# A weighted sum of experts on one core: the stores of ten tokens on ScalarE's queue or on SyncE's

## The chip, the cores and the metric

The kernel runs on 1 core of one Trainium2 chip. A core has five engines with instruction streams of their own: TensorE (PE), VectorE (DVE), ScalarE (ACT), GpSimd (POOL) and SyncE (SP). Transfers between the device's memory and the on-chip memory are done by 16 DMA engines; here SP issues them. The metric is the device time of one execution in microseconds (us). Six runs of the kernel before gave a median of 709.88 us, from 709.42 to 710.2.

## The reference

For each of 16 x 1024 tokens there are 8 expert outputs of 512 numbers and 8 weights. The result is the weighted sum over the experts, all in float32.

```python
def setup_inputs():
    batch, seq, n_experts, expert_dim = 16, 1024, 8, 512
    ...

def reference(expert_outputs, combine_weights):
    weights = combine_weights[..., np.newaxis]
    return np.sum(expert_outputs * weights, axis=2).astype(np.float32)
```

That is 268 MB to read and 33.5 MB to write.

## The kernel before

A token of each of the 128 partitions makes one step of the work: 16,384 tokens are 128 per partition, and "token" from here on means one token in all 128 partitions. It has 16 KB per partition to load (2 MB in all) and 2 KB to store (256 KB in all). 120 tokens are done in 12 rounds (`ROUNDS`) of ten (`R`), which a loop of six passes on DVE runs two at a time; the last 8 tokens (`TAIL`) are done apart.

`ring` holds the loaded rows of ten tokens; a round's tokens are loaded in chunks of 4, 4 and 2 (`CHUNKS`), each into the slots of the same tokens of the round before. `acc` holds the sums of twenty tokens, one half for even rounds and one for odd (`h`). The instruction streams are written out by hand, one function for each engine, and ordered by semaphores alone:

- SP, `loads_and_stores` (L94): for each round the three loads (L107), each after DVE has finished the tokens whose slots it overwrites (`done` counts finished tokens), and then, from round 1 on, the store of the round before (`store`, L95 to L100; its transfer is issued at L98), after `done` has reached all of that round's tokens. This is the value for which the third load waited already. Then come the eight single loads of the tail (L119), the store of round 11 (L120), and four stores of the tail's tokens, of 4, 2, 1 and 1 tokens (L123). Transfers of one issuing engine go into one queue.
- ACT, `weights` (L139): a copy of the weights of each round from `w_t`, which holds all of them, to `w_c` (L145), which holds two rounds' worth; from round 2 on after DVE has finished the round whose half is overwritten. Then 32 diagonal matrices for the tail (L150).
- DVE, `terms` (L170): for each round it waits for the weights, for the half of `acc` to be stored (`stored[h]`), and for each chunk's load (all through `take`, L172); then, for pairs of tokens, one product (L203) and seven multiply-adds (L186) for each token. For the tail it adds four terms of each token (L186) to four that PE has summed.
- PE, `first_terms` (L155): for each tail token four products by diagonal matrices, summed in PSUM (L162).
- POOL makes an identity matrix, once.

Of the kernel before, what the change touches and what calls it, by code (L numbers as in the profile page):

```python
# [10 lines left out]
def kernel(  # L11
# [17 lines left out]
    nc = tc.nc  # L29
# [6 lines left out]
    R = 10  # L36
# [5 lines left out]
    ROUNDS = LOOP // R  # L42
# [10 lines left out]
    o_g = o[0:cut].rearrange("(n p g) d -> n p g d", p=P, g=G)  # L53
# [17 lines left out]
    acc = one.tile([P, G, D], fp32, name="acc")  # L71
# [10 lines left out]
    stored = [sem(f"stored{h}") for h in range(2)]  # L82
    step = sem("step")
    done = sem("done")
# [6 lines left out]
    def load_of(j):  # L91
        return [k for k, (q, m) in enumerate(tail_loads) if q <= j < q + m][0]

    def loads_and_stores(sync):  # L94
        def store(n):  # L95
            h = n % 2
            sync.wait_ge(done, (n + 1) * R)
            sync.dma_start(  # L98
                out=o_g[n // 2, :, h * R : h * R + R], in_=acc[:, h * R : h * R + R]
            ).then_inc(stored[h], 16)  # L100

        for n in range(ROUNDS):
            for c, (r, m) in enumerate(CHUNKS):
                if n:
                    sync.wait_ge(done, (n - 1) * R + r + m)
                g = n % 2 * R + r
                sync.dma_start(  # L107
                    out=ring[:, r : r + m], in_=x_g[n // 2, :, g : g + m]
                ).then_inc(loaded[c], 16)
                if n == 0 and c == 0:  # L110
                    sync.dma_start(
                        out=w_t[:, 0:LOOP].rearrange("p (n g) e -> p n g e", g=G), in_=w_g
                    ).then_inc(w_in, 16)
                    sync.dma_start(out=w_t[:, LOOP:T_P], in_=w_x).then_inc(w_in, 16)
            if n:
                store(n - 1)
        for k, (j, m) in enumerate(tail_loads):
            sync.wait_ge(done, LOOP - R + j + m)
            sync.dma_start(out=ring[:, j : j + m], in_=x_t[:, j : j + m]).then_inc(tail_in[k], 16)  # L119
        store(ROUNDS - 1)  # L120
        for j, m in tail_stores:
            sync.wait_ge(done, LOOP + j + m)
            sync.dma_start(out=o_t[:, j : j + m], in_=acc[:, j : j + m]).then_inc(tail_out, 16)  # L123
        sync.wait_ge(stored[(ROUNDS - 1) % 2], 16)
        sync.wait_ge(tail_out, 16 * len(tail_stores))

    def identity(gpsimd):
        gpsimd.memset(ident, 0.0).then_inc(id_set, 1)  # L128
        gpsimd.affine_select(  # L129
            out=ident,  # L130
            in_=ident,
            compare_op=mybir.AluOpType.not_equal,
            fill=1.0,
            base=0,
            pattern=[[-1, P]],
            channel_multiplier=1,
        ).wait_op(id_set, 1, "sem-ge").then_inc(id_set, 1)

    def weights(scalar):  # L139
        scalar.wait_ge(w_in, 32)  # L140
        for n in range(ROUNDS):
            if n >= 2:
                scalar.wait_ge(done, (n - 1) * R)
            h = n % 2
            scalar.copy(  # L145
                out=w_c[:, h * R : h * R + R], in_=w_t[:, n * R : n * R + R]
            ).then_inc(w_set[h], 1)
        scalar.wait_ge(id_set, 2)
        for k, (j, e) in enumerate(diags):
            i = scalar.mul(out=diag[:, k % DIAGS], in_=ident, mul=w_t[:, LOOP + j, e : e + 1])  # L150
            i.then_inc(diag_set, 1)
            if k >= DIAGS:
                i.wait_op(product, k - DIAGS + 1, "sem-ge")

    def first_terms(tensor):  # L155
        came = set()
        for k, (j, e) in enumerate(diags):
            if load_of(j) not in came:
                came.add(load_of(j))
                tensor.wait_ge(tail_in[load_of(j)], 16)  # L160
            tensor.wait_ge(diag_set, k + 1)
            tensor.matmul(  # L162
                ps[:, j],
                lhsT=diag[:, k % DIAGS],
                rhs=ring[:, j, e],
                start=e == 0,
                stop=e == pe_e[j] - 1,
            ).then_inc(product, 1)
# [58 lines left out]
            count(i, j, e)  # L227

    with tc.tile_critical(no_gpsimd_drain=True):  # L229
        loads_and_stores(nc.sync)  # L230
        identity(nc.gpsimd)
        weights(nc.scalar)
        first_terms(nc.tensor)
        terms(nc.vector)

# [29 lines left out]
```

## Time and profile before

| | |
|---|---|
| median of 6 runs | 709.88 us (709.42 to 710.2) |
| the profiled execution | 709.67 us |
| its span, first to last instruction | 707.9 us |
| DMA engines, mean rate over the span | 427 GB/s |
| loads L107, issue to landing | 22.0 to 50.9 us, median 33.4 |
| stores L98, issue to landing | 30.7 to 39.5 us, median 38.7 |
| tail loads L119, issue to landing | 30.1 to 35.0 us, median 32.5 |

A row of the next table is a group of instructions of one line and form: line, engine, operation, output<-inputs, count | busy us, mean ns of one | idle time just before them, and what ended most of it.

```profile
L186 DVE SCALAR_TENSOR_TENSOR acc<-ring,w_c,acc 128x512 f32<-128x512 f32 x840 | 561.4, 745 | 0.0
L203 DVE TENSOR_SCALAR acc<-ring,w_c 128x512 f32<-128x512 f32 x120 | 52.6, 480 | 65.8 <-DVEq L172 65.8
L162 PE MATMUL ps<-ring,diag 128*128 128x512 f32 x64 | 32.5, 660 | 666.7 <-DMA ring<-in_expert_outputs_dram 666.7
L145 ACT COPY w_c<-w_t 128x80 f32<-128x80 f32 x12 | 3.0, 257 | 556.9 <-DVE acc L186 534.6
L150 ACT ACTIVATE diag<-ident,w_t 128x128 f32<-128x128 f32 x32 | 12.4, 399 | 119.5 <-PE ps L162 119.5
```

DVE's 840 and 120 instructions are the rounds; a pair of tokens takes some 10.06 us, a round of ten 50.3 us. Idle time of an engine that is not the bottleneck costs nothing. SPq and DVEq stand for the instruction queues of SP and DVE, where waits and issues are seen. The trace also keeps a record of every DMA packet (queue, size, start, duration) and of each of the 16 steps by which a transfer counts its semaphore up when it lands, one for each DMA engine.

### The profile page before, as it was taken

Reading aid. Unit: us, or ns where it says so; the run is one execution under the profiler, and the core shown is the slowest. Engines: PE = TensorE matmul, PEld = TensorE weight load, DVE = VectorE, ACT = ScalarE, POOL = GpSimd, SP = SyncE. Lnnn points to the kernel's source line nnn. Section 1 sums busy time; section 2 is a strip of 40 time slices with the busy share of each in tenths; the row PEclk is TensorE's granted clock in tenths of the full one; section 3 lists DMA queues with packets and bytes.
Section 4 is the critical chain, followed back from the end, with each engine's and each line's share of the span. In section 5 each row is a group of like instructions: output and inputs, shape, how many; then the busy total and the mean of one; then the engine's idle time right before and its main releaser. Section 6 shows DMA issues by size and latency. Waiting matters only on the chain. (4 is left out here: it accounts for less than half of the span.)

```text
span 707.9 us, 1388 instructions
## 1 busy us (share of the span) xinstructions
PE 32.5 (5%) x64; PEld 12.9 (2%) x64; DVE 628.1 (89%) x992; ACT 16.6 (2%) x45; POOL 0.7 (0%) x6
## 2 busy tenths in 40 slices
PE   0000000000000000000000000000000000000674
PEld 0000000000000000000000000000000000000221
DVE  0599999899799799799799799799799799899974
ACT  0000000000000000000000000000000000000230
POOL 0000000000000000000000000000000000000000
PEclk9999999999999999999999999999999999999998
DMA  9999999999999999999999999999999999999997
GB/s 411 389 471 418 415 421 438 463 396 463 422 411 448 430 420 454 444 411 448 415 431 435 455 407 459 418 420 439 441 420 450 437 413 446 426 424 427 431 424 302
DMA packets 9570, 302.53 MB, mean 427 GB/s; under 512 B 1120, under 2 KB 1888, under 8 KB 2272
## 3 DMA queue, kind: packets, MB, share of 16 engines
q1 hardware_dynamic: 9568, 302.52, 99.3%
q14 instruction: 2, 0.02, 0.0%
HBM read 268.96 MB, written 33.55 MB: 427 GB/s over the span
## 5 line engine op out<-in xcount | busy, mean ns | idle before, releaser
L186 DVE SCALAR_TENSOR_TENSOR acc<-ring,w_c,acc 128x512 f32<-128x512 f32 x840 | 561.4, 745 | 0.0
L203 DVE TENSOR_SCALAR acc<-ring,w_c 128x512 f32<-128x512 f32 x120 | 52.6, 480 | 65.8 <-DVEq L172 65.8
L162 PE MATMUL ps<-ring,diag 128*128 128x512 f32 x64 | 32.5, 660 | 666.7 <-DMA ring<-in_expert_outputs_dram 666.7
L162 PEld LDWEIGHTS ps<-ring,diag 128*128 128x128 f32 x64 | 12.9, 211 | 685.4 <-DMA ring<-in_expert_outputs_dram 671.5
L186 DVE SCALAR_TENSOR_TENSOR acc<-ring,w_t,acc 128x512 f32<-128x512 f32 x24 | 17.6, 750 | 0.6
L145 ACT COPY w_c<-w_t 128x80 f32<-128x80 f32 x12 | 3.0, 257 | 556.9 <-DVE acc L186 534.6
L150 ACT ACTIVATE diag<-ident,w_t 128x128 f32<-128x128 f32 x32 | 12.4, 399 | 119.5 <-PE ps L162 119.5
L186 DVE SCALAR_TENSOR_TENSOR acc<-ring,w_t,ps 128x512 f32<-128x512 f32 x8 | 5.9, 745 | 7.8 <-PE ps L162 7.8
L145 ACT ACT_TABLE_LOAD x1 | 1.3, 1283 | 0.9 <-SPq L229 0.9
L129 POOL TENSOR_SCALAR_AFFINE_SELECT ident<-ident 128x128 f32<-128x128 f32 x1 | 0.3, 292 | 0.1
L128 POOL MEMSET ident<- 128x128 f32 x1 | 0.2, 204 | 0.5 <-SPq L229 0.5
L249 POOL MEMSET const-bfloat16-1.0<- 128x1 bf16 x1 | 0.1, 102 | 0.0
L249 POOL MEMSET const-uint8-127<- 128x1 uint8 x1 | 0.1, 102 | 0.0
L249 POOL MEMSET const-float32-0.0<- 128x1 f32 x1 | 0.1, 99 | 0.2 <-issue 0.2
L249 POOL MEMSET const-float32-1.0<- 128x1 f32 x1 | 0.1, 99 | 0.0
## 6 DMA issues: line engine op xcount, KB each, us to landing
ring<-in_expert_outputs_dram SPq DMA_DIRECT2D x12, 4096.0 KB, 33.0
out_dram<-acc SPq DMA_DIRECT2D x12, 2560.0 KB, 38.7
ring<-in_expert_outputs_dram SPq DMA_DIRECT2D x8, 2048.0 KB, 32.5
out_dram<-acc SPq DMA_DIRECT2D x1, 1024.0 KB, 19.1
out_dram<-acc SPq DMA_DIRECT2D x1, 512.0 KB, 9.4
out_dram<-acc SPq DMA_DIRECT2D x2, 256.0 KB, 5.4
w_t<-in_combine_weights_dram SPq DMA_DIRECT2D x1, 480.0 KB, 22.7
ring<-in_expert_outputs_dram SPq DMA_DIRECT2D x24, 33.7
```

Source lines behind the costliest of these rows:

```text
L128: gpsimd.memset(ident, 0.0).then_inc(id_set, 1)
L129: gpsimd.affine_select(out=ident, in_=ident, compare_op=mybir.AluOpType.not_equal, fill=1.0, base=0, pattern=[[-1, P]], channel_multiplier ...
L145: scalar.copy(out=w_c[:, h * R : h * R + R], in_=w_t[:, n * R : n * R + R]).then_inc(w_set[h], 1)
L150: i = scalar.mul(out=diag[:, k % DIAGS], in_=ident, mul=w_t[:, LOOP + j, e : e + 1])
L162: tensor.matmul(ps[:, j], lhsT=diag[:, k % DIAGS], rhs=ring[:, j, e], start=e == 0, stop=e == pe_e[j] - 1,).then_inc(product, 1)
L186: return vector.scalar_tensor_tensor(out=acc[:, g], in0=ring[:, g % R, e], scalar=weight, in1=before, op0=mult, op1=add)
L203: i = vector.tensor_scalar_mul(out=acc[:, g], in0=ring[:, g % R, 0], scalar1=weight)
L249: nc = _bacc.Bacc("TRN2", target_bir_lowering=False, num_devices=1)
```

## The change

The stores of rounds 0 to 10 move from SP's stream to ACT's. `store` becomes a function of the queue. On ACT, the store of round n-2 stands ahead of the copy of round n's weights and takes over its wait (the same value of `done`); the store of round 10 stands after the last copy and ahead of the diagonal matrices. On SP the loads of all rounds and of the tail now follow one another, and behind them are the store of round 11 and the four stores of the tail, 18 tokens in all, as before. Waits, transfers, their sizes and the work of the other engines are the same.

```diff
-    def loads_and_stores(sync):
-        def store(n):
-            h = n % 2
-            sync.wait_ge(done, (n + 1) * R)
-            sync.dma_start(
-                out=o_g[n // 2, :, h * R : h * R + R], in_=acc[:, h * R : h * R + R]
-            ).then_inc(stored[h], 16)
-
+    def store(queue, n):
+        h = n % 2
+        queue.wait_ge(done, (n + 1) * R)
+        queue.dma_start(
+            out=o_g[n // 2, :, h * R : h * R + R], in_=acc[:, h * R : h * R + R]
+        ).then_inc(stored[h], 16)
+
+    def loads_and_last_stores(sync):
...
-            if n:
-                store(n - 1)
...
-        store(ROUNDS - 1)
+        store(sync, ROUNDS - 1)
...
-    def weights(scalar):
+    def weights_and_stores(scalar):
         scalar.wait_ge(w_in, 32)
         for n in range(ROUNDS):
             if n >= 2:
-                scalar.wait_ge(done, (n - 1) * R)
+                store(scalar, n - 2)
             h = n % 2
             scalar.copy(
                 out=w_c[:, h * R : h * R + R], in_=w_t[:, n * R : n * R + R]
             ).then_inc(w_set[h], 1)
+        store(scalar, ROUNDS - 2)
         scalar.wait_ge(id_set, 2)
```

More of the change, by code (lines that the diff above doesn't have):

```diff
@@ L229 @@
     with tc.tile_critical(no_gpsimd_drain=True):
-        loads_and_stores(nc.sync)
+        loads_and_last_stores(nc.sync)
         identity(nc.gpsimd)
-        weights(nc.scalar)
+        weights_and_stores(nc.scalar)
         first_terms(nc.tensor)
```

## The prediction

> **What bounds the kernel now.** I read the page's first parts, then the waits, the chain of waits, the timeline around one store, and last the DMA packet records. From the page, in order: span; busy time by engine; DMA busy share in 40 slices; DMA queues; DMA issues with KB and us to landing.
>
> ```profile
> span 707.9 us, 1388 instructions
> PE 32.5 (5%) x64; PEld 12.9 (2%) x64; DVE 628.1 (89%) x992; ACT 16.6 (2%) x45; POOL 0.7 (0%) x6
> ...
> DMA  9999999999999999999999999999999999999997
> ...
> q1 hardware_dynamic: 9568, 302.52, 99.3%
> ...
> ring<-in_expert_outputs_dram SPq DMA_DIRECT2D x12, 4096.0 KB, 33.0
> out_dram<-acc SPq DMA_DIRECT2D x12, 2560.0 KB, 38.7
> ```
>
> The DMA engines are the bound: 99.3% of the span is packets of one queue. DVE has 80 us to spare. A transfer lands 33 to 39 us after its issue, so it spends most of that behind others.
>
> The waits (us in total, times, longest) show where DVE's slack lies, and that ACT is idle:
>
> ```profile
> DVE acc L203 <- DVEq L172: 65.8, 11, 25.1
> ...
> DVE acc L186 <- PE ps L162: 7.8, 4, 4.1
> ...
> ACT w_c L145 <- DVE acc L186: 534.6, 10, 54.8
> ```
>
> 25.1 us is the first load; the other 40.7 us are one wait of about 4.1 us in each of ten rounds, ended by the load of tokens 0 to 3.
>
> The chain of waits (start, us, what) at its end:
>
> ```profile
> 660.78 34.68 DMA ring<-in_expert_outputs_dram
> 695.46 0.04 issue
> 695.50 3.71 PE ps L162 x8
> ...
> 701.60 0.75 DVE acc L186
> ```
>
> The end hangs on the last tail load, at 695.46; PE, DVE and the last store's 4.1 us follow.
>
> The timeline around the store of round 10:
>
> ```profile
> 616.33 0.33 SPq L107 DMA_DIRECT2D ring<-in_expert_outputs_dram  x1
> 616.70 0.43 SPq L98 DMA_DIRECT2D out_dram<-acc  x1
> 620.39 0.88 DVE L203 TENSOR_SCALAR acc<-ring,w_c 128x512 f32<-128x512 f32 x2 [4.09 <-DVEq L172]
> ```
>
> At the store's issue three loads stand ahead of it: the last 3.6 us of tokens 0-3 of round 11 (landing at 620.25), tokens 4-7 (639.61) and 8-9 (649.31). The store landed at 655.39.
>
> The packet records give the price of one row on one engine: 2418 ns for 64 KB (chunks of four tokens), 1213 for 32 KB, 761 for a store's 20 KB row, 611 for 16 KB. Each transfer is 8 rows per engine. All are near 27 GB/s an engine, in either direction, and they stand end to end.
>
> **The change, part by part.**
>
> *Removed from SP, added to ACT:* 11 store issues of 432 ns and their 11 waits. SP waits 583 us of the span anyway. ACT gains 11 x 0.43 = 4.8 us against 534.6 us of idle. Queued behind each wait is the copy of w_c, which before waited for the same value of `done`; it starts 0.43 us later, needed some 50 us later: 0. The diagonals now stand behind the store of round 10 (616.7 instead of 561.97); PE first needs them at 660.29: 0, while 43 us of cover last. POOL, PE and DVE issue the same.
>
> *Bytes:* the same 302.5 MB. Stores 0 to 10 are done before the last load in either kernel. Loads plus these stores are what the engines do until 695.46, so order alone leaves that moment where it is: 0.
>
> *Where the stall goes:* the store now starts at 616.7 instead of some 649. Its 8 rows x 0.76 = 6.1 us fall into the load of tokens 4-7, which had 640.53 - 639.61 = 0.9 us to spare on DVE, so DVE waits some 5 us there. The next round's tokens 0-3 land as before, so the 4.1 us wait at L203 vanishes: one wait for another, and DVE runs some 5 us later. At the end DVE idles 7.8 us on PE before the last token, which takes up the 5. Without that cover each us over 7.8 would count fully. Later DVE means later load issues: when DVE has finished tokens 0-3 and frees their slots, the 5 us of tokens 4-7 that it then waits for and 9.7 us of tokens 8-9 (649.31 - 639.61) are still queued, 14.7 us (before: 9.7 + 6.1 of the store, less 0.9). When it frees tokens 4-7, the next round's tokens 0-3 still have some 9 us to go (14 before). So the engines do not run dry: 0. If they did, each us of it would count fully. The 18 late tokens' stores stay on SP: 0.
>
> *What the trace does not show:* two long transfers on two queues taking turns on an engine. The Trainium skill, page "DMA: Bandwidth & Descriptors", section "Queues, rings and completion order", says that an engine takes turns between the queues by packet. If a record is such a packet, each store makes 8 switches to and fro in place of one; no row here shows that. The same page's "Rules for kernel authors" speaks against this change: spreading DMAs over SP and ACT brings no bandwidth, they interleave on the same engines. Read as free interleaving, that makes the time 709.9.
>
> My own count is 8 pairs of switches for each store, 7 more than now, 77 in all, because rows alternate if both queues are served alike. Rows for one pair:
> - Same queue, load to store to load: from the landing of tokens 0-3 in round 8 to that in round 11, three periods. The first engine to land took 54.45 us a round, the eighth 54.50. Packets alone are 16 x 2418 + 8 x 1213 + 8 x 761 + 4 x 9 ns, less 3.5 ns overlap each: 54.39. A pair costs 0.06 to 0.11 us. Over nine rounds from round 2 the last engine lost 0.25.
> - Other queue: twice an instruction fetch of queue 14 (309 and 333 ns) cut into the load stream. The next load packet took 1835 instead of 1213 ns and 1273 instead of 611: 0.62 to 0.66 us lost besides the fetch itself.
>
> Low end for a pair: a gain, if the second queue fills what switches now cost the last engine, 0.25 x 11 = 2.8 us. Overlap of both directions is not excluded either. High end: 0.64 x 88 = 56 us. I take 0.08, the late rounds of the same pair of transfers, since those are the very operations, and a fetch into instruction memory is not. 77 x 0.08 = 6.2 us.
>
> **Sum:** span 707.9 and what lies around it 1.8 make this execution's 709.67; the median is 709.88, 0.2 higher. 709.9 + 0 + 0 + 6.2 = 716.1; I say 716.
>
> **Rivals.**
> - *Free turns:* the rule as read above, or the store served only after the queued loads, so that the change does nothing. For it: the same rate in both directions and no gaps. Against: both pairs of rows show some loss, and 1.4 us over 88 turns is only 0.016 us each. Time 709.9, 708.5 to 711.3.
> - *The other side, the second queue fills the engines' losses:* at the last load the first engine ended at 691.29, the last at 695.46. Of these 4.2 us some 3 grew at the switches up to round 11 (the first engine landed that round's tokens 0-3 at 617.04, the last at 620.25). If one queue moves while the other turns, 2.8 us go: 707. If reads and writes overlap on an engine, more: 11 x 6.06 = 66.7 us of store packets. It decides from 2% overlap of those (1.4 us). With all hidden DVE binds: 25.1 to its start, 12 rounds of five pairs at 10.06 (the timeline's 630.47 to 640.53), 23.5 of tail, 4.1 for the last store and 3.2 from its landing at 706.4 to 709.67 = 660. Against: equal rates of load and store look like one shared path.
> - *Dear turns:* each return to the load queue costs what it cost after the fetch, 709.9 + 56 = 766, or half of that, 738. For it: the only two rows in which a queue was left and resumed. Against: both were fetches, and may be slow at their own target.
>
> **How the numbers follow.** A run of this kernel ranges from 709.42 to 710.2, so 0.2% (1.4 us) is about what can be told from no change. Cheap turns (711.3 to 722): 0.42. Dear or half-dear turns (above 722): 0.20. Free turns or nothing done: 0.13. Filled or overlapped: 0.25. So faster 0.25, same 0.13, slower 0.62. The likeliest case by itself spans 711.5 to 722. The range goes down to 706.5, which takes in the 2.8 us, and leaves some 0.07 for real overlap below; up to 735, which leaves some 0.13 for dear turns above.
>
> **What would show it.** Store to landing: 38.7 us before; with alternating rows some 8 x (2.42 + 0.76) = 25 us, with equal bytes some 12. DVE's wait: about 5 us at tokens 4-7 instead of 4.1 at tokens 0-3, its sum little changed when turns are cheap. Load packets next to store packets longer than 2418 ns or with gaps: their sum over 16 engines is my 6.2 us. A first-to-last spread at the last load below 4.2 us speaks for the filled losses; a span under 706 for overlap. I am wrong if the DMA share falls well below 99% (engines run dry), or if the end no longer hangs on the last tail load but on DVE.

## The result and the profile after

The changed kernel takes 708.24 us (median of 18 runs, 707.74 to 708.81); the kernel before took 709.86 us in the same comparison (38 runs, 709.25 to 710.2). The ratio is 0.9978, with a 95% interval of 0.9972 to 0.9984: 1.6 us faster, just past what can be told from no change. I had forecast 716, some 6 us slower. The profiled execution took 708.63 us, against 709.67 before.

From the page of the changed kernel: span, busy time by engine, DMA busy share, DMA queues, and DMA issues with KB and median us to landing.

```profile
span 706.8 us, 1388 instructions
PE 31.0 (4%) x64; PEld 12.2 (2%) x64; DVE 628.1 (89%) x992; ACT 16.7 (2%) x45; POOL 0.7 (0%) x6
...
DMA  9999999999999999999999999999999999999997
...
q1 hardware_dynamic: 7984, 273.68, 89.8%
q10 hardware_dynamic: 1584, 28.84, 9.5%
...
out_dram<-acc ACTq DMA_DIRECT2D x11, 2560.0 KB, 25.9
```

The engines are as full as before, now from two queues (89.8 + 9.5 = 99.3%). A store lands 25.9 us after its issue instead of 38.7. The time to look for is 1 us in 707, so it will not be found in shares.

DVE's waits in the changed kernel (us in total, times, longest):

```profile
DVE acc L202 <- DVEq L171: 69.1, 13, 25.0
DVE acc L185 <- PE ps L161: 3.4, 2, 1.8
```

Without the first load's 25.0 us DVE waits 44.1 us in the rounds (40.7 before) and 3.4 in the tail (7.8). The timeline around the store of round 10 shows where:

```profile
619.83 0.33 SPq L107 DMA_DIRECT2D ring<-in_expert_outputs_dram  x1
619.84 0.36 ACTq L97 DMA_DIRECT2D out_dram<-acc  x1
...
643.96 0.88 DVE L202 TENSOR_SCALAR acc<-ring,w_c 128x512 f32<-128x512 f32 x2 [4.01 <-DVEq L171]
```

Load and store are now issued in the same moment by two engines. DVE's wait of 4 us stands 24 us behind the store, at tokens 4 to 7, no longer right behind it, at tokens 0 to 3. The chain of waits at the end of the changed kernel (start, us, what):

```profile
664.21 30.17 DMA ring<-in_expert_outputs_dram
694.37 0.04 issue
694.42 3.71 PE ps L161 x8
...
700.52 0.75 DVE acc L185
```

The last tail load lands at 694.37 instead of 695.46. That is 1.1 us, the whole difference between the spans. Everything behind it is the same.

The packet records say why it lands earlier. Packets that follow one another on one engine, found by matching each start to an end (bytes, start in us, ns), show the turns:

```
65536 137.915  2418
20480 140.329   761
65536 141.087  2418
20480 143.501   761
65536 144.258  2418
20480 146.672   761
```

One row of a load, one row of a store, each as long as it is alone and each starting as the one ahead of it ends (they overlap by 4 ns). This is the rule that I cited of the Trainium skill ("DMA: Bandwidth & Descriptors", "Queues, rings and completion order"); the "packet" of its turns is here a single row, 64 KB or 20 KB. I call "loss" what packets take beyond the usual time of their size, summed over all packets and divided by 16 engines. The last load's landing is given for the eighth and the last of the 16 engines.

| profiled execution | loss 73 to 127 us (first store) | loss 127 to 660 us | last load, eighth engine | last engine |
|---|---|---|---|---|
| before | 0.34 | 1.39 | 692.22 | 695.46 |
| before_again | 0.39 | 1.16 | 691.94 | 695.39 |
| after | 0.53 | 0.41 | 691.32 | 694.37 |
| after_again | 0.44 | 0.41 | 691.16 | 694.76 |

The first engine to land its last load, at 691.0 to 691.3 us, is hardly moved. The others had fallen behind it at the stores, and hardly do any more once the first store is past. In the round of the first store both kernels lose, the changed one on 64 KB rows beside the first store rows that took up to 3076 ns instead of 2418; no run shows why.

### The profile page after: what moved, and what is told of

It is laid out like the page before. It is cut to its first block, busy times and chain, and to the rows that moved or that the text cites. A ratio compares the mean times of both kernels' runs of the same rounds, so it can differ in the third digit from the quotient of the medians.

```text
span 706.8 us, 1388 instructions
## 1 busy us (share of the span) xinstructions
PE 31.0 (4%) x64; PEld 12.2 (2%) x64; DVE 628.1 (89%) x992; ACT 16.7 (2%) x45; POOL 0.7 (0%) x6
## 3 DMA queue, kind: packets, MB, share of 16 engines
q1 hardware_dynamic: 7984, 273.68, 89.8%
## 5 line engine op out<-in xcount | busy, mean ns | idle before, releaser
L161 PE MATMUL ps<-ring,diag 128*128 128x512 f32 x64 | 31.0, 631 | 667.1 <-DMA ring<-in_expert_outputs_dram 667.1
## 6 DMA issues: line engine op xcount, KB each, us to landing
out_dram<-acc ACTq DMA_DIRECT2D x11, 2560.0 KB, 25.9
```

The costliest lines, as they stand in the source:

```text
L161: tensor.matmul(ps[:, j], lhsT=diag[:, k % DIAGS], rhs=ring[:, j, e], start=e == 0, stop=e == pe_e[j] - 1,).then_inc(product, 1)
```

## The experiments

Three theories stood at the start: the loss is paid at the ends of a burst of store rows (1), by sharing the loads' queue (2), or the gain comes from the moment of the store (3). A burst is the unbroken run of store rows that one store puts on an engine. "Beside" gives the median of the kernel before in the same comparison, and ratios are to it. In the edits, `...` marks lines left out, among them the counts that DVE and SP wait for where a store is made of more transfers.

**rows_one_queue**: the turns of the changed kernel, but in one queue.

```diff
...
+                    for p in range(0, P, 16):
+                        sync.dma_start(
+                            out=ring[p : p + 16, r : r + m], in_=x_g[n // 2, p : p + 16, g : g + m]
+                        ).then_inc(loaded[c], 16)
+                        if n:
+                            piece(n - 1, p)
...
```

> Stores 0 to 10 stay on SP's queue, but each, and the load of tokens 8 and 9 issued with it, is cut into 8 transfers of 16 partitions (one row for each DMA engine), issued in turns: row order load, store, load, store in one queue. Theory 1 (the loss is paid at the ends of a burst of store rows and vanishes when rows take turns, whatever the queue): as with two queues, 708.2 to 708.8. Theory 2 (the loss is paid because the store stands in the loads' own queue, where its landing holds up the load behind it): at least 709.9, up to 8 times the loss at the end of a store, some 0.15 x 8 x 11 = 13 us more. Theory 3 (the gain comes from the moment in the round at which the store moves): 709.9.

948.06 to 1004.56 us in six runs (median 965.78), beside 709.69; the ratio of the two fastest is 1.345 (1.339 to 1.352). No theory had that. The transfers of 16 partitions are slow themselves: in the first round, where no store runs, the 32 KB rows of this load took some 4.4 us instead of 1.21. It fits the Trainium skill ("DMA: Bandwidth & Descriptors", "The descriptor swizzle"), by which the engines of a 128-partition transfer each write a port of their own; no run here shows the ports. So the run says nothing on the theories.

**two_bursts**: one queue, twice as many bursts, each half as long.

```diff
...
+            a = h * R + 5 * k
+            sync.wait_ge(done, n * R + (8 if k == 0 else R))
...
+                if n and c:
+                    store(n - 1, c - 1)
-            if n:
-                store(n - 1)
...
```

> The kernel before, with each store of rounds 0 to 11 cut into tokens 0-4, issued behind the load of tokens 4-7, and tokens 5-9, issued behind the load of tokens 8 and 9: all on SP, two bursts of store rows a round in place of one. Rows of 10 KB cost some 385 ns by the rows of 20, 16 and 8 KB (761, 611, 309), so 16 x 385 - 8 x 761 = 72 ns a store, 0.8 us in all. Theories 1 and 2 (each burst costs a loss at its ends, in the mean 1.7 us an engine over the rounds before): twice the ends, 709.9 + 0.8 + 1.7 = 712.4. Theory 3: half of the store moves earlier, 709.9 + 0.8 - 0.8 = 709.9 or a little less.

709.69 us beside 709.69, ratio 1.0002 (0.9989 to 1.0015). Not 712.4: the loss did not double. From 127 to 660 us it fell to 0.48, about as much less as the smaller rows cost by the expectation. A second execution:

> two_bursts once more, for its packet records: if a burst of half the length loses less, the engines lose 0.3 to 0.7 us in the mean from 127 to 660 us again; if the first record was a chance, 1.2 or more.

It lost 0.54 us in that stretch (one execution, 710.01 us). So theories 1 and 2 as I had put them, a price for each burst, are wrong.

**halves_on_act**: twice as many turns.

```diff
...
+        for a in (h * R, h * R + 5):
+            queue.dma_start(
+                out=o_g[n // 2, :, a : a + 5], in_=acc[:, a : a + 5]
+            ).then_inc(stored[h], 16)
...
```

> The changed kernel, with every store of ten tokens cut into two of five on the same queue: 16 rows of 10 KB for each engine and store instead of 8 of 20 KB, so twice as many turns between the queues. Theory 1 (turns are free): 708.2 + 0.8 us of smaller rows = 709.0. The price of my prediction (0.08 us a turn): 88 more turns, 708.2 + 0.8 + 7 = 716.

707.80 us, ratio 0.9978 (0.9966 to 0.9991), the same as the changed kernel's. 88 more turns on each engine cost nothing that can be seen; the loss from 127 to 660 us was 0.08 us. The packets of one engine (bytes, start in us, ns) show that the turns were taken:

```
65536 240.936  2418
10240 243.350   385
65536 243.731  2418
10240 246.146   385
```

This is the run that settles my prediction's price.

**late_on_act**: the same turns, four tokens later.

```diff
-        queue.wait_ge(done, (n + 1) * R)
+        queue.wait_ge(done, (n + 1) * R + (4 if n < ROUNDS - 1 else 0))
```

> The changed kernel, with each store on ACT's queue issued only when DVE has finished four more tokens (some 20 to 24 us later), so that its rows fall beside the loads of tokens 8 and 9 and the next round's 0-3 instead of beside tokens 4-7. Theories 1 and 2: the moment is nothing, 708.2 (707.7 to 708.8); DVE waits at tokens 0-3 again. Theory 3: the time goes back to 709.9.

707.94 us, ratio 0.9977 (0.9964 to 0.9989). Of the two moments tried, neither is better; theory 3 falls.

**early_in_queue**: one whole burst, other neighbours.

```diff
-                if n:
+                if n and c == 2:
+                    store(n - 1)
+                elif n:
...
-            if n:
-                store(n - 1)
```

> The kernel before, all on SP, with the store of round n-1 placed ahead of the load of tokens 8 and 9 instead of behind it (both wait for the same count): one burst of 20 KB rows, one queue, other neighbours. If any whole burst in the loads' queue pays (some 0.15 us an engine and round): 709.7 as before. If the loss belongs to the neighbours of the burst (32 KB rows ahead, 64 KB rows behind, the next round's load waiting): near the changed kernel, 708.2 to 708.6.

709.48 us beside 709.52, ratio 0.9999 (0.9990 to 1.0008); loss from 127 to 660 us 0.96. A whole burst in the loads' queue pays in both places tried.

**three_bursts**: one queue, finer still.

```diff
...
+                if c == 2:
+                    for k in range(2):
+                        if n:
+                            store(n - 1, k)
+                        sync.dma_start(
+                            out=ring[:, r + k], in_=x_g[n // 2, :, g + k]
+                        ).then_inc(loaded[c], 16)
+                    if n:
+                        store(n - 1, 2)
+                    continue
...
```

> All on SP: each store in three bursts (tokens 0-3, 4-6, 7-9), the load of tokens 8 and 9 as two loads between them. Smaller rows cost some 0.12 us a round, 1.3 in all. Theory A (a long burst in the loads' queue loses, finer bursts lose less): from 127 to 660 us the engines lose less in the mean than the 0.48 us of two_bursts (before: 1.2 to 1.4), time 710.0 to 710.4. Theory B (each burst in the loads' queue loses its own): 1.2 us or more in that stretch, 711 or more.

709.86 us beside 710.01, ratio 1.0001 (0.9992 to 1.0010), and a loss of 0.29 us from 127 to 660 us: theory A. In one queue the loss falls as the bursts get finer, 0.96 to 1.39, then 0.48 and 0.54, then 0.29. In three_bursts smaller rows eat the gain: the first engine to land its last load did so at 692.28 us, 1.0 later than in the kernel before. A second queue is not needed to lose less, so standing in the loads' queue (theory 2) is not the price by itself; the second queue gave fine turns without smaller rows.

**before_again** and **after_again**: second sets of records, in the table above.

> The kernel before once more, for a second set of packet records. If the loss is its own: from 73 to 660 us each engine loses 1.4 to 2.0 us in the mean to packets longer than their usual time, most of them next to or at the end of a store's burst, 0.07 or more in every round. If the first record was a chance: near the changed kernel's 0.9 us, 0.05 or less a round after the first.

> The changed kernel once more, for its packet records: a loss in the first store's round (0.4 to 0.8 us), then 0.05 us or less a round, 0.3 to 0.5 us from 127 to 660 us. If the first record was a chance: over 1 us in that stretch.

Both as expected (709.61 and 709.01 us, one execution each); in the kernel before, each round lost 0.07 us or more, in the changed kernel each round from the second store on 0.05 or less.

**all_on_act**: the store of round 11 among the tail's loads.

```diff
-        store(sync, ROUNDS - 1)
...
+            if k == 12:
+                store(scalar, ROUNDS - 1)
```

> The changed kernel, with the store of round 11 on ACT's queue too, so that only the last 8 tokens' stores stay behind the loads. If the end is what the slowest DMA engine still has to move, until the last tail token's own chain is later: the last load lands 6.1 us later at 700.4, PE 3.7, DVE 3.1 and some 1.9 us for the last store give 709.2, and 1.5 + 1.8 us follow: 712.5. If the last store costs 4.1 us by itself: 714.7. If order is nothing: 708.2.

712.26 us, ratio 1.0040 (1.0025 to 1.0056). Its chain of waits:

```profile
663.66 36.20 DMA ring<-in_expert_outputs_dram
699.86 0.04 issue
699.90 3.71 PE ps L162 x8
...
706.00 0.75 DVE acc L186
```

The last load lands 5.5 us later than in the changed kernel. The last store, issued at 706.78, landed at 708.78, in 2.0 us: so its 4.1 us in the kernel before were not its own. Against the changed kernel (ratio 0.9978) this move costs some 4 us: the store of round 11 is better left behind the loads, where the engines still have it to do while PE and DVE finish.

**fetch_early**: DVE's two instruction fetches moved.

```diff
...
+        for _ in range(64):
+            vector.sem_inc(pad, 1)
```

> The changed kernel, with 64 extra instructions on DVE ahead of the loop (each counts up a semaphore that nobody reads; DVE waits 25 us for the first load there anyway). The two instruction fetches of queue 14, at 51.4 and 681.9 us, each hold one DMA engine up by some 0.95 us, and it is the last at the end. If they are DVE's (128 instructions apart in its stream), the first moves to the start, ahead of the load rows, the second into the loop, and none falls into the tail: the slowest engine ends 0.95 us earlier, 707.3. If they belong to another engine, or the extra instructions only add a fetch: 708.2 or more.

708.30 us, ratio 0.9983 (0.9974 to 0.9992): no gain. The fetches did move, to 10.2 and 103.0 us, so they are DVE's. But both still fall among the loads. The slowest engine landed its last load at 693.85, in the range of the other runs with whole stores on ACT (693.79 to 694.76).

**fifths_on_act**: five transfers of two tokens for each store.

```diff
...
+        for a in range(h * R, h * R + R, 2):
+            queue.dma_start(
+                out=o_g[n // 2, :, a : a + 2], in_=acc[:, a : a + 2]
+            ).then_inc(stored[h], 16)
...
```

> The changed kernel, with every store of ten tokens cut into five of two tokens on the same queue: 40 rows of 4 KB for each engine and store, 440 turns an engine. A 4 KB row took 159 ns, so rows cost 40 x 155.5 - 8 x 757.5 = 0.16 us more a store, 1.8 us in all. Turns free, small rows paid: 708.2 + 1.8 = 710.0. Turns free and the small rows' overhead hidden by the other queue: 708. My prediction's 0.08 us a turn: 708.2 + 1.8 + 352 x 0.08 = 738.

803.89 us, ratio 1.132 (1.130 to 1.134), for a reason that I had not thought of. From its page (DMA busy tenths), its timeline and its landings of the output:

```profile
DMA  9999999929999947999983999992999996599998
```

```profile
414.36 0.88 DVE L203 TENSOR_SCALAR acc<-ring,w_c 128x512 f32<-128x512 f32 x2 [27.41 <-DVEq L172]
```

```profile
DMA to landing us min/median/max: 4.3/31.2/80.3
```

The DMA engines run dry several times. 40 rows of a store, each behind a load row of 2.42 us, need up to 40 x (2.42 + 0.16) = 103 us, and DVE needs the half of `acc` back after 54. So it waits at L172 for `stored` (the last of five transfers landed at 414.11, DVE went on at 414.36), finishes no tokens, and no loads are issued. The price per turn can't be read from this run.

## Why the prediction was wrong, step by step

- *The bound.* Right: the DMA queues' share is 99.3% in both kernels, and what this change moved is what the engines lose.
- *Everything priced at nothing.* Right: ACT's issues are 11 x 0.36 us in its idle time, and the engines did not run dry. The DVE wait moved from tokens 0-3 to tokens 4-7 with 4.0 us where I had said some 5, DVE finished the rounds 3.4 us later (674.16 against 670.74), and the tail's idle time fell from 7.8 to 3.4 us and took that up.
- *Rows in turns, a store landing in some 25 us.* Right: 25.9 us.
- *The step that failed* is "I take 0.08, the late rounds of the same pair of transfers ... 77 x 0.08 = 6.2 us". I read the loss at the ends of a store burst as the price of a switch and multiplied it by the number of switches. halves_on_act doubled the turns and took 707.80 us, and once the first store was past, a load row next to a store row of the other queue took its usual 2418 ns. The changed kernel lost 0.41 us from 127 to 660 us, so a turn costs at most 0.41 / 80, some 0.005 us. What I had measured is a property of the burst, eight store rows on all 16 engines at about the same time; it shrinks as the burst is cut (three_bursts), where my reading would have had it grow. The records of the kernel before show as much: 0.44 of its 1.39 us fell on the 32 KB rows, which stand ahead of the store and so ahead of any switch. The rival "free turns" therefore had the price of a turn right, and the time wrong by the loss that it left in place.
- *The high end, 0.62 us after an instruction fetch.* The price is the fetch's: it is there in the changed kernel too (a 16 KB row behind the fetch at 681.9 took 1273 ns). Beside store rows, load rows came near it only in the round of the first store; from 127 to 660 us its longest 64 KB row took 2516 ns.
- *The rival that held* is the one on the faster side, "the second queue fills the engines' losses", at 707. Its size was too large: it counted on 2.8 us of the last engine's loss, and the medians show 1.6, the profiled executions 1.0 and 0.6. Of the 3 us that it put to the switches, 1.0 was there before the first store (tokens 0-3 of round 1 landed at 72.27 on the first engine, at 73.31 on the last), and at round 11 the changed kernel's engines were still 2.2 us apart, not 3.2. Its mechanism, that one queue moves while the other turns, is not shown: finer bursts in one queue lose less as well.
- *"The end hangs on the last tail load, at 695.46; PE, DVE and the last store's 4.1 us follow."* Half right. In the kernel before, the slowest engine has the store rows of all 18 late tokens left when its last load lands: 8 x 0.761 + 8 x 0.309 + 8 x 0.159 + 16 x 0.084 = 11.2 us of packets, and the last store lands at 706.43. On the other engines that store had landed by 704.4. So the end was the slowest engine's backlog, and PE and DVE had some 2 us to spare. all_on_act, where the backlog is gone, shows the store's own 2.0 us.

Open: what it is in a whole burst that holds engines up was not tried, nor why both kernels lost 0.3 to 0.5 us in the round of their first store, nor whether equal turns in one queue would do as well as two queues; the run for that was spoilt by its transfers of 16 partitions. Nor is it clear why the medians differ by 1.6 us when the profiled executions differ by 1.0 and 0.6; both of the changed kernel's lie above its median of 708.24.

No version beat the changed kernel beyond the intervals: halves_on_act (0.9978) and late_on_act (0.9977) are its equals. Little is left. In the changed kernel eight engines land the last load within 0.2 us of the first (691.16 to 691.32); the last is 3.2 us behind, and 1.9 us of that are the two fetches (0.31 + 0.62 and 0.33 + 0.66).

## What to carry to other kernels

Here the DMA engines were full from end to end, and stores moved to another queue gained only what the engines lost on their packets; look for that in packet durations and in the spread of the 16 landings, not in the waits. That held as long as the engines did not run dry (fifths_on_act) and the last stores stayed behind the loads (all_on_act). A loss seen at a transition is not yet a price per transition: double the number of transitions before multiplying. Where two queues take turns row by row, a store of many small rows beside a load of long rows lands late, so compare rows x (long row + small row) with the time until its buffer is needed.

## What the runs showed of the hardware that I had not expected

- Two queues took turns by single rows, 64 KB against 20 KB, with no gap: packets end to end, each at its usual duration once the first store was past. The packet of 4 bytes (9 ns) that counts a load's semaphore up took a turn of its own.
- An instruction fetch of 8 KB on queue 14 (0.31 us) made the next load row on that engine 0.62 to 0.66 us longer. Here one engine caught both fetches, and it ended last.
- A transfer of 16 neighbouring partitions moved 32 KB rows in some 4.4 us each instead of 1.21.
